# Hi and lo token parts side by side: one 512-column product in the gate and up stage of a decoder layer, Trainium2, one core

## The chip, the cores and the metric

The kernel runs on one core of a Trainium2 chip. The metric is the device time of one execution in microseconds (us). Matrix products run on TensorE (PE; PEld are its weight loads), elementwise work on VectorE (DVE) and ScalarE (ACT); GpSimd (POOL) and SyncE (SP) issue most transfers.

## What is computed

One decoder layer, float32, 512 tokens, width 1024: three token mixers, their gated merge, and a SwiGLU feed-forward part. The change lies in the feed-forward part (F = 2816):

```python
h = h + rms_norm(mix, ln_mix_post)
u = rms_norm(h, ln_ffn_pre)
a = silu(u @ w_gate) * (u @ w_up)          # 1024 -> F, twice
ffn = a @ w_down                           # F -> 1024
h = h + rms_norm(ffn, ln_ffn_post)
```

## The kernel before

Precision. Each float32 matrix x is split into two fp32r tiles: hi is a cast of x by ACT, lo = x - hi by DVE (`split`). A product is three matmuls into one PSUM place: hi hi, hi lo, lo hi (`mm3`).

Seven products. Gate and up products, and the down products behind them, are done on 2 x 2 quarters with seven products in place of eight. The token factors B11, T1, N2, N22, T3, B21, T4 (`fac`; sums and differences of the quarters of the normed tokens) are made once, by `place`. The weights are streamed: the feed-forward width is cut into HF = 11 blocks n, and in each block the products p1, p5, p6, p3, p7, p2, p4 (`PROD`) form one **unit** each: 128 x 1024 weights, that is 2 output groups j of 4 chunks k. Each of these 8 places is an `mm3` of 256 token columns, 24 matmuls a unit (`gu`). j = 0 and 1 fill the two halves of one PSUM bank of 512 columns. p1, p6, p7, p4 add up in the block's bank x, p5 and p3 in y, p2 in w.

A unit's end (`g_end`). After p1, p5 and p6 ACT copies the bank to SBUF (`snap`). After p3, p7 and p2 one DVE op joins the bank with such a copy (`join`). After p4 the activation reads the bank itself. Each finished quarter goes through `act_out`: Silu on ACT (`sg`), a DVE multiply with the up half (`aq`). After all blocks 42 down units follow, with products of 512 columns (`down`, `dn_mm`, `dn_issue`, `dn_sum`).

Order. Weights are loaded by DMAs (SP, some POOL with accumulation), split some units ahead, and multiplied (`Stream`, `fs`). What each engine runs in which order is a table, `ORDER`; `PLAN` gives each tile its place in SBUF or PSUM, so that a reused place makes the next writer wait. All instructions go through one recorder and so carry one line number, L209 (`Noted`). `mix` adds the residual to the mixed tokens: xr = x + mixed, one tile of 128 tokens at a time; xr stays in SBUF up to the end of the kernel, where `dn_half` adds it.

In the trace names lose their numbers: gp is a snapped gate product, hi and lo are the parts of the streamed weights, raw and wide what they are made of. As in the kernel, "block 3" is n = 3.

Of the kernel before, what the change touches and what calls it, by code (L numbers as in the profile page):

```python
# [32 lines left out]
WARM = 10  # L33

# [2027 lines left out]
```

## Time and profile before

| | before |
|---|---|
| time, median of 3 runs (lowest to highest) | 779.85 us (779.32 to 780.1) |
| profiled execution: span, its only own time | 777.5 us |
| PE busy | 769.8 us, 99% |
| DVE busy | 623.0 us, 80% |
| ACT busy | 488.4 us, 63% |
| matmuls and weight loads on PE | 4614 and 4614 |
| gate and up units of blocks 3 to 10 | 504.96 to 666.24 us |
| down units and the last chain | 666.24 us to the end |

The span runs from the first to the last instruction of the one profiled execution; the runs were timed without the profiler and hold what lies around the span too. An engine's busy share is a mean over stages with different limits, so the stage of the change is read by windows and timelines. In a timeline the durations of neighbouring matmuls overlap; what one costs is the step from its start to the next start.

### The profile page before, as it was taken

Reading aid. Unit: us, or ns where it says so; the run is one execution under the profiler, and the core shown is the slowest. Engines: PE = TensorE matmul, PEld = TensorE weight load, DVE = VectorE, ACT = ScalarE, POOL = GpSimd, SP = SyncE. Lnnn points to the kernel's source line nnn. Section 1 sums busy time; section 2 is a strip of 40 time slices with the busy share of each in tenths; the row PEclk is TensorE's granted clock in tenths of the full one; section 3 lists DMA queues with packets and bytes.
Section 4 is the critical chain, followed back from the end, with each engine's and each line's share of the span. In section 5 each row is a group of like instructions: output and inputs, shape, how many; then the busy total and the mean of one; then the engine's idle time right before and its main releaser. Section 6 shows DMA issues by size and latency. Waiting matters only on the chain.

```text
span 777.5 us, 12379 instructions
## 1 busy us (share of the span) xinstructions
PE 769.8 (99%) x4614; PEld 677.3 (87%) x4614; DVE 623.0 (80%) x1003; ACT 488.4 (63%) x881; POOL 100.5 (13%) x133
## 2 busy tenths in 40 slices
PE   9999999999999999999999999999999999999996
PEld 6899888778888888878888899999999999888885
DVE  7994787677787757999898599877776869997776
ACT  7662776678585659778944486455455555766752
POOL 3000421003112020011012001100000000215000
PEclk9999999999999999999999999999999999999999
DMA  8444988248569696478899349877777654949602
GB/s 304 145 127 121 318 258 264 82 154 191 117 138 205 149 200 203 109 193 187 304 341 267 63 109 261 212 181 187 188 190 188 183 146 150 191 103 240 131 1 108
DMA packets 46940, 140.14 MB, mean 180 GB/s; under 512 B 5600, under 2 KB 7184, under 8 KB 46816
## 3 DMA queue, kind: packets, MB, share of 16 engines
q1 hardware_dynamic: 31344, 88.35, 33.8%
q0 software_dynamic: 15104, 50.61, 33.5%
q8 instruction: 36, 0.59, 0.3%
q10 hardware_dynamic: 432, 0.39, 0.2%
q14 instruction: 24, 0.20, 0.1%
HBM read 132.51 MB, written 13.11 MB: 187 GB/s over the span
## 4 chain that ended last, share of the span: by engine, by line
PE 99%; DVE 0%; issue 0%; DVEq 0%; ACT 0%
PE p L209 99%; DVE fg L209 0%; DVEq L2050 0%; DVE s L209 0%; DVE wide L209 0%; ACT sqr L209 0%; DVE eps_t L209 0%
## 5 line engine op out<-in xcount | busy, mean ns | idle before, releaser
L209 DVE TENSOR_TENSOR lo<-raw,hi 128x1024 fp32r<-128x1024 f32 (+3 forms) x140 | 162.5, 1167 | 48.7 <-ACT hi L209 47.4
L209 ACT CAST hi<-raw 128x1024 fp32r<-128x1024 f32 (+3 forms) x140 | 140.5, 1011 | 91.7 <-PE p L209 66.1
L209 ACT CAST hi<-wide 128x1024 fp32r<-128x1024 f32 (+1 forms) x58 | 59.2, 1020 | 54.1 <-PE p L209 27.9
L209 DVE TENSOR_TENSOR lo<-wide,hi 128x1024 fp32r<-128x1024 f32 (+1 forms) x58 | 68.7, 1185 | 17.1 <-ACT hi L209 16.9
L209 PE MATMUL p<-lo,lh 128*128 128x512 f32 x154 | 59.9, 389 | 0.0
L209 PE MATMUL p<-hi,ll 128*128 128x512 f32 x154 | 59.6, 389 | 0.0
L209 PE MATMUL p<-hi,lh 128*128 128x512 f32 x154 | 59.0, 389 | 0.0
L209 PE MATMUL p<-lo,uh 128*128 128x512 f32 (+1 forms) x160 | 57.2, 358 | 0.0
L209 PE MATMUL p<-hi,ul 128*128 128x512 f32 (+1 forms) x160 | 57.0, 358 | 0.0
L209 PE MATMUL p<-hi,uh 128*128 128x512 f32 (+1 forms) x160 | 56.7, 360 | 0.0
L209 PE MATMUL p<-uh,hi 128*128 128x512 f32 x136 | 54.5, 400 | 0.0
L209 PE MATMUL p<-uh,lo 128*128 128x512 f32 x136 | 53.2, 391 | 0.0
L209 PE MATMUL p<-ul,hi 128*128 128x512 f32 x136 | 53.0, 391 | 0.0
L209 POOL DMA_DIRECT2D raw<-in_w_g x24 | 21.0, 879 | 136.8 <-DVE lo L209 109.8
L209 PEld LDWEIGHTS p<-hi,ll 128*128 128x128 f32 x154 | 28.9, 188 | 6.0
L209 PEld LDWEIGHTS p<-lo,lh 128*128 128x128 f32 x154 | 28.9, 188 | 6.0
L209 PEld LDWEIGHTS p<-hi,lh 128*128 128x128 f32 x154 | 28.9, 188 | 5.9
L209 PEld LDWEIGHTS p<-hi,uh 128*128 128x128 f32 x160 | 30.0, 188 | 4.5 <-ACT gq2p L209 0.3
L209 PEld LDWEIGHTS p<-hi,ul 128*128 128x128 f32 x160 | 30.0, 188 | 3.8
L209 PEld LDWEIGHTS p<-lo,uh 128*128 128x128 f32 x160 | 30.1, 188 | 3.6
L209 PEld LDWEIGHTS p<-uh,hi 128*128 128x128 f32 x136 | 25.6, 188 | 6.0 <-issue 0.7
L209 PEld LDWEIGHTS p<-uh,lo 128*128 128x128 f32 x136 | 25.5, 188 | 5.3
(724 smaller groups left out, 2417.7 us busy)
## 6 DMA issues: line engine op xcount, KB each, us to landing
wide<-in_w_gu SPq DMA_DIRECT2D x30, 512.0 KB, 4.7
raw<-in_w_gu SPq DMA_DIRECT2D x27, 512.0 KB, 5.4
raw<-in_w_g POOLq DMA_DIRECT2D x24, 512.0 KB, 6.4
raw<-in_w_g SPq DMA_DIRECT2D x18, 512.0 KB, 4.8
raw<-in_w_p SPq DMA_DIRECT2D x14, 512.0 KB, 5.5
wide<-in_w_gu POOLq DMA_DIRECT2D x14, 512.0 KB, 6.7
raw<-in_w_gu POOLq DMA_DIRECT2D x13, 512.0 KB, 7.6
bp<-in_w_dn SPq DMA_DIRECT2D x22, 256.0 KB, 6.1
```

Source lines behind the costliest of these rows:

```text
L209: ins = f(*args, **kw)
```

## The change

In blocks 3 to 10 a place is two matmuls and not three. The hi and lo tile of each token factor now lie side by side in one tile of 1024 columns (`pair`). The hi part of the weights multiplies 256 columns of the hi tile and 256 of the lo tile in one product of 512 columns, written to two halves of a bank ("main" and "rest"); the lo part of the weights then multiplies the hi columns into main. j = 0 and 1 take a bank each, so a group of products has two banks (`banks`), and the eight banks make four such pairs. Blocks 0 to 2 and the down units keep `mm3`.

At a unit's end ACT copies main (p1, p5, p6 and now p4), and a DVE op adds rest to the copy. A join (p3, p7, p2) becomes two DVE ops, one with main, one with rest, the second reading what the first wrote. p4's activation reads the copy.

To make room in SBUF, xr is written to DRAM by SP after `mix` (`put_away`, 8 writes of 256 KB) and read back in the down stage (`get_back`, 8 reads); the weights of p3 and p7 of the first three down chunks become one tile of 1024 columns, loaded by one transfer and added by one DVE op; two sets of kept products of an earlier stage lie in a spare place. `ORDER` and `PLAN` are new tables.

The core of the diff:

```diff
+    def banks(name):
+        return places.take(psa, "p2", [P, 1024], F32, name)
...
+    def pair(name):
+        t = places.take(ckp, "ck2", [P, 1024], F32R, name)
+        return t[:, :512], t[:, 512:], t[:, :].rearrange("p (s n) -> p s n", s=2)
+
...
+    def put_away(t):
+        away[t] = [drm.tile([P, 512], F32, name=f"h{t}{h}") for h in range(2)]
+        for d, x in zip(away[t], hres[t]):
+            nc.sync.dma_start(d[:, :], x[:, :])
+
+    def get_back(t):
+        hres[t] = [ck(f"hr{t}{h}") for h in range(2)]
+        for d, x in zip(away[t], hres[t]):
+            nc.sync.dma_start(x[:, :], d[:, :])
+
...
     RIGHT = ("B11", "B21", "T1", "N2", "N22", "T3", "T4")
-    fac = {r: Late(lambda c, r=r: (ck(f"{r}h{c}", F32R), ck(f"{r}l{c}", F32R))) for r in RIGHT}
...
+    def banked(n, b):
+
+        return n >= 3
+
+    def halves(ps, i):
+        return ps.rearrange("p (j s n) -> p s j n", j=2, s=2)[:, i]
+
...
         def snap():
             t = ck(f"g{p}{n}")
-            ins = nc.scalar.copy(t[:, :], ps[:, :])
+            ins = nc.scalar.copy(seen(t), main)
             if "behind" in st:
                 after(ins, st["behind"][0])
+            if wide:
+                nc.vector.tensor_tensor(seen(t), seen(t), rest, op=ALU.add)
             gk[(n, p)] = t
-
-        def join(t, x, y, op, i, j):
-            ins = nc.vector.tensor_tensor(t[:, :], x[:, :], y[:, :], op=op)
-            if "behind" in st:
-                after(ins, st["behind"][1])
+            return t
+
+        def join(t, sign, i, j):
+            if sign > 0:
+                ordered_dve(nc.vector.tensor_tensor(seen(t), main, seen(t), op=ALU.add))
+            else:
+                ordered_dve(nc.vector.tensor_tensor(seen(t), seen(t), main, op=ALU.subtract))
+            if wide:
+                nc.vector.tensor_tensor(seen(t), seen(t), rest, op=ALU.add if sign > 0 else ALU.subtract)
             act_out(n, i, j, t[:, :256], t[:, 256:])
 
         if p in ("p1", "p5", "p6"):
             snap()
         elif p == "p3":
-            t = gk.pop((n, "p6"))
-            join(t, t, ps, ALU.subtract, 1, 0)
+            join(gk.pop((n, "p6")), -1, 1, 0)
         elif p == "p7":
-            t = gk.pop((n, "p5"))
-            join(t, t, ps, ALU.subtract, 1, 1)
+            join(gk.pop((n, "p5")), -1, 1, 1)
         elif p == "p2":
-            t = gk.pop((n, "p1"))
-            join(t, ps, t, ALU.add, 0, 0)
+            join(gk.pop((n, "p1")), 1, 0, 0)
+        elif wide:
+            snap()
+            t = gk.pop((n, "p4"))
+            act_out(n, 0, 1, t[:, :256], t[:, 256:], -1.0)
         else:
             act_out(n, 0, 1, ps[:, :256], ps[:, 256:], -1.0)
...
         def gen(hi, lo):
             b = G_BANK[p]
+            wide = banked(n, b)
             if p in ("p1", "p5", "p2"):
-                gb[(n, b)] = dps(f"gw{n}") if b == "w" else aps(f"g{b}{n}")
+                gb[(n, b)] = banks(f"g{b}{n}") if wide else dps(f"gw{n}") if b == "w" else aps(f"g{b}{n}")
             ps = gb[(n, b)]
             for j in range(2):
                 for k in range(4):
-                    r = cols(fac[G_RIGHT[p]][k // 2], (k % 2) * 256, 256)
-                    first = p in ("p1", "p5", "p2") and j == 0 and k == 0
-                    mm3(ps[:, j * 256 : (j + 1) * 256], cols((hi, lo), (j * 4 + k) * P, P), r, first, k == 3)
+                    f = fac[G_RIGHT[p]][k // 2]
+                    begins = p in ("p1", "p5", "p2") and k == 0
+                    w = cols((hi, lo), (j * 4 + k) * P, P)
+                    r = cols(f, (k % 2) * 256, 256)
+                    if wide:
+                        o = ps[:, j * 512 : (j + 1) * 512]
+                        both = f[2][:, :, (k % 2) * 256 : (k % 2 + 1) * 256]
+                        mm(o.rearrange("p (s n) -> p s n", s=2), w[0], both, begins, False)
+                        mm(o[:, :256], w[1], r[0], False, k == 3)
+                    else:
+                        mm3(ps[:, j * 256 : (j + 1) * 256], w, r, begins and j == 0, k == 3)
                 yield 1.44
             g_end(p, n, ps)
...
+            else:
+                rb[(p, c)] = rb.pop(("p3", c))
+                nc.gpsimd.dma_start(rb[(p, c)][:, :], src, accum_op=ALU.add)
...
+                t = rb[("p3", c)]
+                nc.vector.tensor_tensor(rr[c][:, :], rr[c][:, :], t[:, :], op=ALU.add)
+                return
             for i, t in enumerate(rb[("p3", c)]):
...
+
+    for t in range(NT):
+        load_at(len(seq) + units.index(("p2", 1 if t < 2 else 5)), get_back, t)
```

The order on PE at the first product of block 3 (out<-moving, stationary operand as the order prints them: bank0 is PSUM, pair5 the two parts of B11). Before:

```order
L209 MATMUL p1_105<-B11h0_4032,hi3_79 128x256
L209 MATMUL p1_105<-B11l0_4033,hi3_79 128x256
L209 MATMUL p1_105<-B11h0_4032,lo3_83 128x256
L209 MATMUL p1_105<-B11h0_4032,hi3_79 128x256
L209 MATMUL p1_105<-B11l0_4033,hi3_79 128x256
L209 MATMUL p1_105<-B11h0_4032,lo3_83 128x256
```

and in the changed kernel:

```order
L215 MATMUL bank0_104<-pair5_110,hi3_79 128x512
L215 MATMUL bank0_104<-pair5_110,lo3_83 128x256
L215 MATMUL bank0_104<-pair5_110,hi3_79 128x512
L215 MATMUL bank0_104<-pair5_110,lo3_83 128x256
L215 MATMUL bank0_104<-pair3_108,hi3_79 128x512
L215 MATMUL bank0_104<-pair3_108,lo3_83 128x256
```

Two matmuls, of 512 and 256 columns, stand where three of 256 stood.

The order on DVE at the start of block 4 (gpPN is product P of block N: gp14 is p1, gp54 p5, gp64 p6; lo are the parts of the next units' weights; ll1, sq, sr belong to the down products). Before:

```order
L209 TENSOR_TENSOR lo0_80<-raw0_72,hi1_77 128x1024
L209 TENSOR_TENSOR lo2_82<-wide0_84,hi0_76 128x1024
L209 TENSOR_TENSOR lo3_83<-wide0_84,hi3_79 128x1024
L209 TENSOR_TENSOR lo1_81<-wide0_84,hi2_78 128x1024
L209 TENSOR_TENSOR gp64_5186<-gp64_5186,p2_106 128x512
L209 TENSOR_TENSOR lo0_80<-raw1_73,hi1_77 128x1024
```

and in the changed kernel:

```order
L215 TENSOR_TENSOR lo0_80<-wide0_84,hi1_77 128x1024
L215 TENSOR_TENSOR gp14_4982<-gp14_4982,bank0_104 128x512
L215 TENSOR_TENSOR lo2_82<-raw0_72,hi0_76 128x1024
L215 SCALAR_TENSOR_TENSOR aq011_4791<-gp43_4952,sg301_4955 128x256
L215 TENSOR_TENSOR ll1_6096<-aq001_4759,lh1_6095 128x512
L215 TENSOR_TENSOR lo3_83<-wide0_84,hi3_79 128x1024
L215 TENSOR_TENSOR gp54_5005<-gp54_5005,bank0_104 128x512
L215 TENSOR_TENSOR sq1_4958<-aq101_4695,aq111_4728 128x512
L215 TENSOR_TENSOR sr1_4961<-sq1_4958,aq001_4759 128x512
L215 TENSOR_TENSOR gp64_5028<-gp64_5028,bank0_104 128x512
L215 TENSOR_TENSOR lo1_81<-wide0_84,hi2_78 128x1024
L215 TENSOR_TENSOR gp64_5028<-gp64_5028,bank0_104 128x512 x2
```

Before, DVE has nothing to do at the ends of p1, p5 and p6; its first op on block 4's banks is the join that follows p3 (gp64). Now the adds of rest for gp14, gp54 and gp64 stand between the splits, with the squares and the multiply of block 3 before and behind them, and the join is two ops.

The order on SP, where the first weights of the gate and up stage are loaded. Before:

```order
L209 DMA bc_g_fpre1_3691<-in_g_fpre 128x512
L209 DMA raw0_72<-in_w_gu 128x1024
L209 DMA raw2_74<-in_w_gu 128x1024
L209 DMA raw1_73<-in_w_gu 128x1024
L209 DMA raw3_75<-in_w_gu 128x1024
L209 DMA wide0_84<-in_w_gu 128x1024 x5
L209 DMA raw0_72<-in_w_gu 128x1024
```

and in the changed kernel:

```order
L215 DMA raw0_72<-in_w_gu 128x1024
L215 DMA wide0_84<-in_w_gu 128x1024 x4
L215 DMA h00_3755<-xr00_3597 128x512
L215 DMA h01_3756<-xr01_3598 128x512
L215 DMA wide0_84<-in_w_gu 128x1024
L215 DMA raw3_75<-in_w_gu 128x1024
L215 DMA h10_3868<-xr10_3601 128x512
L215 DMA h11_3869<-xr11_3602 128x512
L215 DMA h20_3955<-xr20_3605 128x512
L215 DMA h21_3956<-xr21_3606 128x512
```

The writes of xr (h00 to h31) stand between the loads.

## Rows read from the trace of the kernel before

**Rows 1.** The page, part 1: busy time, share of the span and instructions of each engine.
```profile
PE 769.8 (99%) x4614; PEld 677.3 (87%) x4614; DVE 623.0 (80%) x1003; ACT 488.4 (63%) x881; POOL 100.5 (13%) x133
```

**Rows 2.** The chain of waits in order of time: start us, us, what.
```profile
1.35 769.81 PE p L209 x4613
```

**Rows 3.** Windows: stretch us, its length, busy us of each engine, PEclk, DMA share, GB/s.
```profile
504.96:646.08 141.12, 141.12 (x1179) 141.12 (x1178) 105.55 (x125) 72.24 (x101) 10.48 (x12) 1.00 0.66 176
666.24:771.16 104.92, 104.91 (x464) 86.54 (x462) 87.27 (x141) 67.11 (x117) 18.25 (x21) 1.00 0.56 123
```

**Rows 4.** DVE groups in 504.96 to 666.24: busy us, mean ns | idle before, releasers.
```profile
L209 DVE TENSOR_TENSOR lo<-wide,hi 128x1024 fp32r<-128x1024 f32 x31 | 37.9, 1224 | 15.6 <-ACT hi L209 15.5
L209 DVE TENSOR_TENSOR lo<-raw,hi 128x1024 fp32r<-128x1024 f32 x26 | 31.8, 1225 | 13.7 <-ACT hi L209 13.7
```

**Rows 5.** PE timeline, block 2: start us, us, engine line op out<-in.
```profile
480.00 0.28 PE L209 MATMUL p<-N22h,hi 128*128 128x256 f32 x1
480.12 0.28 PE L209 MATMUL p<-N22l,hi 128*128 128x256 f32 x1
```

**Rows 6.** PE timeline, products of 512 columns, an earlier stage.
```profile
199.99 0.39 PE L209 MATMUL p<-hi,y10h 128*128 128x512 f32 x1
...
201.12 0.39 PE L209 MATMUL p<-hi,y11l 128*128 128x512 f32 x1
```

**Rows 7.** PE timeline, moving operand of two runs (qas).
```profile
176.80 0.28 PE L209 MATMUL p<-kas,qas 128*128 128x256 f32 x1
...
177.39 0.28 PE L209 MATMUL p<-kal,qas 128*128 128x256 f32 x1
```

**Rows 8.** DVE timeline, block 3.
```profile
523.18 0.68 DVE L209 TENSOR_TENSOR gp<-p,gp 128x512 f32<-128x512 f32 x1
523.78 0.68 DVE L209 TENSOR_TENSOR sq<-aq,aq 128x512 f32<-128x512 f32 x1
524.45 1.23 DVE L209 TENSOR_TENSOR lo<-raw,hi 128x1024 fp32r<-128x1024 f32 x1
525.59 0.42 DVE L209 TENSOR_TENSOR aq<-gp,sg 128x256 f32<-128x256 f32 x1
525.93 0.42 DVE L209 SCALAR_TENSOR_TENSOR aq<-p,sg 128x256 f32<-128x256 f32 x1
```

**Rows 9.** ACT timeline from the end of the T1 product, 551.04, of block 5.
```profile
551.12 1.05 ACT L209 CAST hi<-raw 128x1024 fp32r<-128x1024 f32 x1 [0.97 <-PE p L209]
552.07 0.58 ACT L209 COPY gp<-p 128x512 f32<-128x512 f32 x1
```

**Rows 10.** DVE timeline of the same place.
```profile
552.20 1.23 DVE L209 TENSOR_TENSOR lo<-raw,hi 128x1024 fp32r<-128x1024 f32 x1 [0.79 <-ACT hi L209]
```

**Rows 11.** A join of block 2: the next unit on PE, and the join on DVE.
```profile
499.20 0.28 PE L209 MATMUL p<-B21h,hi 128*128 128x256 f32 x1
...
499.40 0.69 DVE L209 TENSOR_TENSOR gp<-gp,p 128x512 f32<-128x512 f32 x1 [0.36 <-PE p L209]
```

**Rows 12.** The first gate products on PE, and DVE beside them.
```profile
442.77 0.39 PE L209 MATMUL p<-B11h,hi 128*128 128x256 f32 x1
...
444.29 0.39 PE L209 MATMUL p<-B11l,hi 128*128 128x256 f32 x1
444.51 0.28 PE L209 MATMUL p<-B11h,lo 128*128 128x256 f32 x1
...
443.81 0.42 DVE L209 TENSOR_TENSOR B11l<-p,B11h 128x256 fp32r<-128x256 f32 x1
```

**Rows 13.** SP loads around the mixing stage, and the first and last residual adds.
```profile
408.95 1.60 SPq L209 DMA_DIRECT2D raw<-in_w_gu  x2
...
453.87 2.40 SPq L209 DMA_DIRECT2D raw<-in_w_gu  x2
...
411.58 1.29 DVE L209 TENSOR_TENSOR xr<-xr,mt 128x512 f32<-128x512 f32 x2
...
445.79 1.28 DVE L209 TENSOR_TENSOR xr<-xr,mt 128x512 f32<-128x512 f32 x2
```

More of the change, by code (lines that the diff above doesn't have):

```diff
@@ L33 @@
 WARM = 10
+PAIRS = 14
+SINGLES = 73 - 2 * PAIRS
 ORDER = {
     "tensor": (
[17 rows of a table removed]
[16 rows of a table added]
     ),
     "vector": (
[32 rows of a table removed]
[33 rows of a table added]
     ),
     "scalar": (
[28 rows of a table removed]
[27 rows of a table added]
     ),
     "gpsimd": (
-        "5-12 16 29-30 4 2-3 0-1 14 13 15 17 22 27 21 20 19 18 23 28 25 24 26 31 33 32 34 39 35 41 40 36 42-43 37 "
-        "47-48 44 38 49-50 45 52 51 53 46 54-65 67 66 68-81 86 82 85 87 83-84 88-111 123-128 119 112-118 120-122"
+        "5-12 16 29-30 4 2-3 0-1 14 13 15 17 22 27 21 20 19 18 23 28 25 24 26 31 33 32 34 39 35 41 40 36 42-43 37 47-48 "
+        "44 38 49-50 45 52 51 53 46 54-65 67 66 68-78 80 79 81-83 86 85 84 87-111 120-125 116 112-115 117-119"
     ),
@@ L125 @@
         "0-14 16-18 15 19-27 32 28-31 33-34 36-38 35 39-52 57 60 53-56 63-64 58-59 61-62 65-94 97-98 95-96 101-102 "
-        "99-100 105-106 103-104 109 107-108 110-218"
[3 rows of a table added]
     ),
@@ L130 @@
     "raw": (
-        "3 2 1 0 3 2 1 0 3 2 1 0 3 2 1 0 3 2 1 0 3 2 1 0 3 2 1 0 3 2 1 0 3 2 1 0 3 2 1 2 1 2 1 0 3 0 3 0 3 2 0 1 3 "
-        "2 0 1 3 2 3 2 3 2 0 3 1 2 0"
+        "3 2 1 0 3 2 1 0 3 2 1 0 3 2 1 0 3 2 1 0 3 2 1 0 3 2 1 0 3 2 1 0 3 2 1 0 3 2 1 2 1 2 1 0 3 0 3 0 3 2 0 1 3 2 0 "
+        "1 3 2 3 2 3 2 0 3 1 2 0"
     ),
     "hi": (
-        "3 2 1 0 3 2 1 0 3 2 1 0 3 2 1 0 3 2 1 0 3 2 1 0 3 2 1 0 3 2 1 0 3 2 1 0 2 3 1 0 2 3 1 0 2 3 1 0 2 3 1 0 2 "
-        "3 1 0 2 3 1 0 2 3 1 0 2 3 1 0 2 3 1 0 2 3 1 0 2 3 1 0 2 3 1 0 2 3 1 0 2 3 1"
+        "3 2 1 0 3 2 1 0 3 2 1 0 3 2 1 0 3 2 1 0 3 2 1 0 3 2 1 0 3 2 1 0 3 2 1 0 2 3 1 0 2 3 1 0 2 3 1 0 2 3 1 0 2 3 1 "
+        "0 2 3 1 0 2 3 1 0 2 3 1 0 2 3 1 0 2 3 1 0 2 3 1 0 2 3 1 0 2 3 1 0 2 3 1"
     ),
     "lo": (
-        "3 2 1 0 3 1 2 0 3 1 2 0 3 1 2 0 3 1 2 0 3 1 2 0 3 1 2 0 3 1 2 0 3 1 0 2 1 3 0 2 1 3 0 2 1 3 0 2 1 3 0 2 1 "
-        "3 0 2 1 3 0 2 1 3 0 2 1 3 0 2 1 3 0 2 1 3 0 2 1 3 0 2 1 3 0 2 1 3 0 2 1 3 0"
+        "3 2 1 0 3 1 2 0 3 1 2 0 3 1 2 0 3 1 2 0 3 1 2 0 3 1 2 0 3 1 2 0 3 1 0 2 1 3 0 2 1 3 0 2 1 3 0 2 1 3 0 2 1 3 0 "
+        "2 1 3 0 2 1 3 0 2 1 3 0 2 1 3 0 2 1 3 0 2 1 3 0 2 1 3 0 2 1 3 0 2 1 3 0"
     ),
     "p": (
[5 rows of a table removed]
[4 rows of a table added]
+    ),
+    "p2": (
+        "0 1 2 3 2 1 0 3 2 3 2 0 1 0 0 3 2 1 0 2 3 3 2 1"
     ),
     "ck": (
[21 rows of a table removed]
[19 rows of a table added]
+    ),
+    "ck2": (
+        "5 3 2 11 7 0 9 13 10 4 12 6 1 8"
     ),
     "s": (
[3 rows of a table removed]
[3 rows of a table added]
     ),
     "spare": (
-        "4 3 2 1 1 4 3 2"
+        "0 1 2 3 4 5 6 7 4 5 0 1"
     ),
     "fraw": (
-        "0 2 1 3 8 7 6 5 4 0 2 1 3 8 0 7 4 5 3 6 1 0 2 8 7 5 6 4 3 1 2 7 0 8 5 4 1 6 3 2 0 5 7 8 4 6 2 1 3 0 7 4 5 "
-        "8 6 1 0 2 3 7 5 6 4"
+        "8 3 1 2 0 6 7 4 5 8 3 1 2 0 8 6 5 7 4 2 1 8 3 0 6 7 2 5 4 1 3 6 8 0 7 5 1 2 4 3 8 7 6 0 5 2 3 1 4 8 6 5 7 0 2 "
+        "1 8 3 4 6 7 2 5 0 1 8"
     ),
     "fhi": (
[3 rows of a table removed]
[3 rows of a table added]
     ),
     "flo": (
[3 rows of a table removed]
[3 rows of a table added]
     ),
@@ L243, in __init__, with open @@
         self.held, self.used = {}, 0
-    def open(self, pool, kind, n, shape):
+    def open(self, pool, kind, n, shape, dt=F32):
         for i in range(n if PLAN else 0):
             key = f"{kind}{i}"
-            self.held[key] = pool.tile(shape, F32, tag=key, name=key, bufs=1)
+            self.held[key] = pool.tile(shape, dt, tag=key, name=key, bufs=1)
     def fixed(self, pool, shape, dt, name):
@@ L265, in take @@
         n = int(next(self.plan[kind]))
+        if kind == "ck" and n < SINGLES:
+            return pool.tile(shape, dt, tag=f"ck{n}", name=name, bufs=1)
         if kind == "ck":
-            return pool.tile(shape, dt, tag=f"ck{n}", name=name, bufs=1)
+            n -= SINGLES
+            return self.held[f"pair{n // 2}"][:, n % 2 * 512 : n % 2 * 512 + 512]
+        if kind == "ck2":
+            return self.held[f"pair{n}"]
+        if kind in ("p", "p2"):
+            return self.held["bank0"][:, n * shape[1] : (n + 1) * shape[1]]
         if kind == "spare":
-            return self.held["wide0"][:, self.spare + n * 512 : self.spare + (n + 1) * 512]
+            o = self.spare + n * 512 + (300 if n > 6 else 0)
+            return self.held["wide0"][:, o : o + 512]
         if kind == "fraw" and n > 3:
@@ L353, in tile_kernel @@
     base = ctx.enter_context(tc.tile_pool(name="base", bufs=1))
-    ckp = ctx.enter_context(tc.tile_pool(name="ckp", bufs=73))
+    ckp = ctx.enter_context(tc.tile_pool(name="ckp", bufs=SINGLES))
     sm = ctx.enter_context(tc.tile_pool(name="sm", bufs=16))
@@ L367, in tile_kernel @@
     places.open(sm, "s", 16, [P, 8])
-    places.open(psa, "p", 8, [P, 512])
+    places.open(psa, "bank", 1, [P, 8 * 512])
+    places.open(ckp, "pair", PAIRS, [P, 1024], F32R)
     def ck(name, dt=F32):
         return places.take(ckp, "ck", [P, 512], dt, name)
+    def pair(name):
+        t = places.take(ckp, "ck2", [P, 1024], F32R, name)
+        return t[:, :512], t[:, 512:], t[:, :].rearrange("p (s n) -> p s n", s=2)
     def small(name, n=4):
@@ L790, in q_end @@
         if p in ("p1", "p5", "p6", "p7"):
-            t = qkeep[(p, i)] = ck(f"gq{b}{p}{i}")
+            t = qkeep[(p, i)] = (spare if b == SWA and p in ("p1", "p6") else ck)(f"gq{b}{p}{i}")
             st["chain"] = nc.scalar.copy(t[:, :], ps[:, :])
@@ L1474, in x_load @@
             nc.sync.dma_start(hres[t][h][:, :], a["x"][t * P : (t + 1) * P, h * 512 : (h + 1) * 512])
+    away = {}
+    def put_away(t):
[6 more added lines that the diff above has]
+            nc.sync.dma_start(x[:, :], d[:, :])
     mixed = {}
@@ L1504, in mix @@
             )
+        put_away(t)
         return tmp
     RIGHT = ("B11", "B21", "T1", "N2", "N22", "T3", "T4")
-    fac = {r: Late(lambda c, r=r: (ck(f"{r}h{c}", F32R), ck(f"{r}l{c}", F32R))) for r in RIGHT}
+    fac = {r: Late(lambda c, r=r: pair(f"{r}{c}")) for r in RIGHT}
     turned = {}
@@ L1532, in place @@
         for c in range(2):
-            h, l = (x[:, :].rearrange("p (k n) -> p k n", k=2)[:, :, o : o + P] for x in fac[name][c])
+            h, l = (x.rearrange("p (k n) -> p k n", k=2)[:, :, o : o + P] for x in fac[name][c][:2])
             v = src[:, c * 256 : (c + 1) * 256].rearrange("p (k n) -> p k n", k=2)
@@ L1644, in tile_kernel, with seen, ordered_dve @@
     G_RIGHT = dict(p1="B11", p5="T1", p6="N2", p3="N22", p7="T3", p2="B21", p4="T4")
+    def banked(n, b):
+        return n >= 3
+    def halves(ps, i):
+        return ps.rearrange("p (j s n) -> p s j n", j=2, s=2)[:, i]
     def g_end(p, n, ps):
+        b = G_BANK[p]
+        wide = banked(n, b)
+        main = halves(ps, 0) if wide else ps[:, :].rearrange("p (j n) -> p j n", j=2)
+        rest = halves(ps, 1) if wide else None
+        def seen(t):
+            return t[:, :].rearrange("p (j n) -> p j n", j=2)
+        def ordered_dve(ins):
+            if "behind" in st:
+                after(ins, st["behind"][1])
         def snap():
             t = ck(f"g{p}{n}")
-            ins = nc.scalar.copy(t[:, :], ps[:, :])
+            ins = nc.scalar.copy(seen(t), main)
             if "behind" in st:
                 after(ins, st["behind"][0])
+            if wide:
+                nc.vector.tensor_tensor(seen(t), seen(t), rest, op=ALU.add)
             gk[(n, p)] = t
-        def join(t, x, y, op, i, j):
-            ins = nc.vector.tensor_tensor(t[:, :], x[:, :], y[:, :], op=op)
-            if "behind" in st:
-                after(ins, st["behind"][1])
+            return t
[6 more added lines that the diff above has]
+                nc.vector.tensor_tensor(seen(t), seen(t), rest, op=ALU.add if sign > 0 else ALU.subtract)
             act_out(n, i, j, t[:, :256], t[:, 256:])
@@ L1684, in gen @@
             b = G_BANK[p]
+            wide = banked(n, b)
             if p in ("p1", "p5", "p2"):
-                gb[(n, b)] = dps(f"gw{n}") if b == "w" else aps(f"g{b}{n}")
+                gb[(n, b)] = banks(f"g{b}{n}") if wide else dps(f"gw{n}") if b == "w" else aps(f"g{b}{n}")
             ps = gb[(n, b)]
@@ L1724, in tile_kernel @@
     LAST = 3
+    RAW3 = 3
     rr = {}
@@ L1751, in dn_issue @@
                 nc.gpsimd.dma_start(rr[c][:, :n], src, accum_op=ALU.add)
+        elif p in ("p3", "p7") and c < RAW3:
+            src = a["w_dn"][:, h, j * HF + ks[0] : j * HF + ks[-1] + 1].rearrange("p k n -> p (k n)")
+            if p == "p3":
+                rb[(p, c)] = places.take(fp, "fraw", [P, 1024], F32, f"q{c}")
+                nc.sync.dma_start(rb[(p, c)][:, :], src)
+            else:
+                rb[(p, c)] = rb.pop(("p3", c))
+                nc.gpsimd.dma_start(rb[(p, c)][:, :], src, accum_op=ALU.add)
         elif p == "p7":
@@ L1762, in add @@
         def add():
+            if c < RAW3:
+                t = rb[("p3", c)]
+                nc.vector.tensor_tensor(rr[c][:, :], rr[c][:, :], t[:, :], op=ALU.add)
+                return
             for i, t in enumerate(rb[("p3", c)]):
```

223 rows, old and new, of tables (ORDER, PLAN) are left out of this document.

## The prediction, before the run

> **What bounds the kernel now.** I read the engine totals, then the chain, then the windows of the stage that the change touches, then single instructions there. PE is busy 99% of the span, DVE 80% [rows 1]. The chain of waits is one piece of PE matmuls, 769.81 us long, with nothing between them [rows 2]. Blocks 3 to 10 run from 504.96 to 666.24, which is 20.16 us a block and 2.88 a unit; in the first seven of them PE fills all 141.12 us at granted clock 1.00, DVE works 105.55 of these and ACT 72.24 [rows 3]. So each ns taken from PE's stream there is worth a ns, until PE has to wait for a bank; DVE, with 5.1 us idle a block, is the next limit. Over the eight blocks 15.6 + 13.7 us of DVE's idle time are waits for ACT's hi cast [rows 4].
>
> **What PE gains.** A matmul of 256 columns starts every 120 ns [rows 5]. One of 512 columns starts every 226.6 ns: from 199.99 to 201.12 are five steps [rows 6]. 256 more columns cost 106.6 ns, so 13.4 ns of each matmul are independent of its length. The change streams the same columns and has one matmul and one weight load fewer in each of 8 blocks x 7 units x 8 places = 448 places: a place takes 226.6 + 120 = 346.6 ns instead of 360. A unit becomes 2.773 us, a block 19.41, and the gain is 448 x 13.3 = **6.0 us**. The new moving operand is two runs, a row of no 512-column product here; the nearest has 256 columns in two runs of 128 (kas times qas) and comes every 116 to 120 ns like the plain ones [rows 7], so I price this form at nothing.
>
> The Trainium skill (TensorE: Matmul & The Clock Gate, section "Wait — 56ns, not 53.3ns?") puts the fixed cost of a warm matmul at about 2.5 ns; by that, an estimate, merging would return only 1.1 us. The two pitches above do not agree with it, and the sum goes by them.
>
> **What DVE and ACT pay.** Each unit's end now leaves two halves in PSUM, and the second needs a DVE add of 512 columns. Such an op lasts 0.68 us, but the next one starts 0.60 after it (523.18, 523.78) [rows 8]. Seven adds a block are 4.2 us; on 15.1 (105.55 over seven) that is 19.3. Counting the changed order's own rows from one p2 join to the next, with pitches 1.14, 0.60 and 0.34 for 1024, 512 and 256 columns [rows 8], gives 18.7 on average: some squares and sums now stand behind the last block. Three of the seven adds (joins of p3, p7, p2) read what the op ahead of them has just written, so they start at its end plus about 0.03: 0.72 instead of 0.60, 0.36 a block. Together **19.05 of 19.41 us**: DVE is full to 98%, where it was 75%. Were the pitch between 0.60 and the whole 0.68 on all 24.7 ops of a block, it would be up to 2.0 more; I take 0.60, since it is measured on this form.
>
> The Trainium skill (VectorE: DVE Perf Modes, section "The DRAIN you can't avoid") says that the next op does not start until the pipe is empty. By that, the upper bound just named would hold and the kernel would be slower (case C below); the rows show starts 0.08 before the previous end, and so do not agree.
>
> ACT gains one copy a block (p4; a copy is 0.58 [rows 9]): 72.24 us of 141.12 become 76 [rows 3], hidden.
>
> **The wait that is added.** A unit's bank pair may be overwritten only when the rest add has read it. Four pairs are in turn, and most products write where one stood two units before. Take a unit that ends at T. ACT casts the next weights first (T+0.08), copies the product from T+1.03 to T+1.61 [rows 9]. DVE stands in its fixed order: lo, which waited for that cast, starts at T+1.16 [rows 10] and holds it 1.14, so the rest add runs from T+2.30 to T+2.98. The next-but-one unit wants the bank at T+2.77: **0.2 to 0.25 us late**. Before, the bank was free at T+1.61, or, for a join, which starts 0.20 after the unit (499.40 for 499.20) [rows 11], at about T+0.9. In the other case of the order shown above, block 4's p5, DVE has lo, the p1 add, lo, a multiply, ll, lo ahead of the add; it gets to it 0.68 late. When PE does wait, its next matmuls also lose about 0.09: 444.29 waits for the DVE op from 443.81 (end 444.23), and 444.51 comes 0.22 later instead of 0.12 [rows 12].
>
> I laid the changed order's rows one behind another with these durations for all eight blocks. A stall at one boundary relieves the next, so they are eleven and not fifty-six: five of 0.24 or 0.25 (p1 and p6 of block 3, p6 of 5, p5 of 7, p1 of 8), two of 0.68 (p5 of 4 and 6), 0.11, 0.09, 0.44 and 0.64 in blocks 8 to 10. That is 3.8 us, and 11 x 0.09 = 1.0: **4.8 us given back**. The order of before, laid in the same way, has no stall, as in the trace. The bounds: nothing, if the adds come a third of an op earlier; and DVE's whole pace, below.
>
> **The rest.** DVE does more behind block 10: it is busy 87.27 of 104.92 us there [rows 3], about 5 more fit, and the laid rows give PE no wait; taken at nothing, and up to 1 us if that work falls into a stretch where DVE is already full. The eight writes of the residual stand in SP's queue among the gate and up loads, each behind its tile's add. Two loads that SP issued at 408.95 now wait for the tile added from 411.58 to 412.87 [rows 13]: 4 us later, against a first gate product at 442.77 [rows 12]; the last writes are ready at 445.79 + 1.28 = 447.07, before SP's next load at 453.87 [rows 13]. Nothing, unless the writes hold up a load that is needed at once; then a few tenths. The reads back are 2 MB in the last 105 us, where the DMAs are busy 0.56 [rows 3]. Fewer, larger bp loads and one add of 1024 (1.14) for two of 512 (1.20) are too small to see. Rows before block 3 are swapped in a few places on DVE; I put -0.3 to +0.6 on that and take nothing.
>
> **Sum.** -5.97 + 4.84 = -1.1. The profiled execution's span of 777.5 becomes 776.4; the median of the runs lies 2.35 above that span, and so the time is **778.7** against 779.85.
>
> **Rivals.** 0.2% is 1.56 us, about what a measurement of this kernel can tell from no change: faster is below 778.29, slower above 781.41.
>
> A. As summed, most of the gain returned as PE waits of 0.1 to 0.7 us. Its own range, 777.0 to 780.6, is stalls of 3.1 to 6.7. Chance 0.48, of which 0.14 is faster, 0.32 the same, 0.02 slower.
>
> B. The adds come in time. For it: the plain case fails by a quarter of a us only, and one early stall relieves those after it; against it: the fixed order puts a 1.14 us lo ahead of each add. With no stall 773.9, with half of them 776.3. Chance 0.28, faster.
>
> C. DVE sets the pace, and the kernel is **slower**. It is 19.05 us busy a block; it waits 5.1 now, 3.7 of it for ACT's cast ((15.6 + 13.7) / 8) [rows 4]. The cast itself waits for PE to free its hi tile, 0.97 us ahead of 551.12 [rows 9], so each PE stall passes to ACT and back to DVE. The same end is reached if the ops take their whole 0.68: 18.7 + 2.0 = 20.7 a block, 784.2. It decides at 20.16 - 19.05 = 1.1 us of idle left a block; my laid rows have 0.96, which is close. With 1.6 left, a block takes 20.65 and the time is 779.85 + 8 x 0.49 = 783.8; range 781.5 to 785. Against it: a DVE that is late finds its inputs ready, and its waits shrink. Chance 0.19.
>
> D. Merging saves little, because 512 columns in two runs lose a few ns at the turn, or the fixed part is not per matmul. If 2 to 3 ns of the 13.4 fall away, 1.1 us are gained; the stalls shrink as the units stay longer, to six of some 0.2: 779 to 780.5. Against it are the pitches of [rows 5, 6, 7]. Chance 0.05, 0.04 the same and 0.01 slower. The Trainium skill's fixed cost, quoted above from TensorE: Matmul & The Clock Gate, would be this case.
>
> **Numbers.** Faster: 0.14 + 0.28 = 0.42. Same: 0.32 + 0.04 = 0.36. Slower: 0.02 + 0.19 + 0.01 = 0.22. The range has to hold most of B and half of C: 774.0 to 782.5.
>
> **What would show it.** In the profile after: matmuls in blocks 3 to 10 alternate 226.6 and 120 ns; units without a wait take 2.77 us; DVE is busy over 18.5 of each 20 us there; PE's gaps, 0.1 to 0.7 us and some eleven in all, stand at unit starts and end when a DVE add on a bank ends, most behind p1, p5 and p6; up to 504.96 and from block 10's end the times are those of before, moved. If a lone 512-column product takes 240 ns, D holds. If PE's gaps sum to under 2 us, B holds. If they sum to over 7.5 with DVE waiting for hi in between, C. I am wrong in another way if the difference lies before 504.96 (a late load) or in the last 105 us.

## The result, and the profile after

| | before | after |
|---|---|---|
| time, median of 7 runs each | 779.65 us | 781.79 us |
| ratio (95% interval) | | 1.0027 (1.0016 to 1.0038) |
| span of the profiled execution | 777.5 us | 779.7 us |
| blocks 3 to 10 | 161.28 us | 161.34 us |

The changed kernel is 0.27% slower; the forecast was 778.7 us, 1.1 us faster. The page's engine totals after, which answer to [rows 1]:

```profile
PE 769.2 (99%) x4166; PEld 653.4 (84%) x4166; DVE 655.9 (84%) x1050; ACT 492.9 (63%) x883; POOL 97.8 (13%) x130
```

PE has 448 matmuls fewer and is still busy for the same time (769.8 us before). The windows after (columns as in [rows 3]): blocks 3 to 10, their first seven, the down units.

```profile
506.22:667.56 161.34, 159.54 (x898) 136.83 (x897) 153.08 (x197) 93.74 (x134) 12.21 (x14) 1.00 0.66 176
506.22:647.60 141.38, 139.77 (x787) 119.87 (x786) 133.40 (x171) 78.37 (x110) 10.47 (x12) 1.00 0.67 179
667.56:772.50 104.94, 104.91 (x464) 86.53 (x462) 91.01 (x142) 63.30 (x106) 15.78 (x18) 1.00 0.61 142
```

The two spans differ by 2.2 us, and the stage of the change has hardly a share in it: it starts 1.26 later (506.22 for 504.96), lasts 0.06 longer; the down units take the same 104.52 to the last matmul (770.76 before, 772.08 after); the end behind that takes 7.62 us for 6.77 (the spans to the hundredth are 779.71 and 777.53). DVE works 133.40 us in seven blocks, 19.06 a block. The chain of waits, one piece before [rows 2], has 167 pieces now. From the start of block 3 and of the last wait of block 4 (start us, us, what):

```profile
504.94 4.17 PE bank L215 x27
509.11 0.02 issue
509.13 1.07 ACT hi L215
510.20 0.02 issue
510.22 1.23 DVE lo L215
511.45 0.61 DVE gp L215
512.06 0.04 issue
512.10 1.44 PE bank L215 x7
...
533.20 0.60 DVE ll L215
533.80 1.14 DVE lo L215
534.93 0.61 DVE gp L215
535.54 0.04 issue
535.59 18.42 PE bank L215 x105
```

The first wait is the plain case of the prediction: p1's unit ends at 509.1, ACT casts, DVE subtracts, then adds rest, and p6's first product starts at 512.10. The second is block 4's p5. PE and DVE timelines there:

```profile
534.17 0.39 PE L215 MATMUL bank<-pair,hi 128*128 128x512 f32 x1
534.40 0.28 PE L215 MATMUL bank<-pair,lo 128*128 128x256 f32 x1
534.51 0.39 PE L215 MATMUL bank<-pair,hi 128*128 128x512 f32 x1
534.75 0.28 PE L215 MATMUL bank<-pair,lo 128*128 128x256 f32 x1
535.59 0.50 PE L215 MATMUL bank<-pair,hi 128*128 128x512 f32 x1 [0.56 <-DVE gp L215]
535.92 0.28 PE L215 MATMUL bank<-pair,lo 128*128 128x256 f32 x1
```

```profile
531.64 1.22 DVE L215 TENSOR_TENSOR lo<-raw,hi 128x1024 fp32r<-128x1024 f32 x1
532.78 0.42 DVE L215 SCALAR_TENSOR_TENSOR aq<-gp,sg 128x256 f32<-128x256 f32 x1
533.11 0.69 DVE L215 TENSOR_TENSOR ll<-aq,lh 128x512 fp32r<-128x512 f32 x1
533.72 1.22 DVE L215 TENSOR_TENSOR lo<-wide,hi 128x1024 fp32r<-128x1024 f32 x1
534.85 0.68 DVE L215 TENSOR_TENSOR gp<-gp,bank 128x512 f32<-128x512 f32 x1
```

That DVE queue is the one the order showed, op for op, and the last product before the wait would end its step at 534.87; the next starts at 535.59. A wait is counted wherever PE's step from one product to the next is over 0.05 us longer than 0.2267 (512 columns) or 0.12 (256 columns); what the steps have above these sums to 4.3 us in the stage. So 4.2 us of PE time were gained (161.28 less 157.1, the stage without its waits) and 4.3 given back.

### The profile page after: what moved, and what is told of

Its sections match the earlier page's. It is cut to its first block, busy times and chain, and to the rows that moved or that the text cites. A ratio compares the mean times of both kernels' runs of the same rounds, so it can differ in the third digit from the quotient of the medians.

```text
span 779.7 us, 11519 instructions
## 1 busy us (share of the span) xinstructions
PE 769.2 (99%) x4166; PEld 653.4 (84%) x4166; DVE 655.9 (84%) x1050; ACT 492.9 (63%) x883; POOL 97.8 (13%) x130
## 4 chain that ended last, share of the span: by engine, by line
PE 90%; DVE 6%; issue 2%; ACT 2%; DVEq 0%
PE bank L215 90%; DVE lo L215 3%; DVE gp L215 2%; DVE wide L215 1%; ACT hi L215 1%; ACT mw L215 0%; DVE aq L215 0%; DVE pair L215 0%; ACT L215 0%; ACT wide L215 0%; ACT pair L215 0%; DVE fg L215 0%; ACT mt L215 0%; DVEq L2136 0%; DVE sq L215 0%
## 5 line engine op out<-in xcount | busy, mean ns | idle before, releaser
L215 PE MATMUL bank<-pair,hi 128*128 128x512 f32 (+1 forms) x1072 | 309.9, 360 | 1.8 <-DVE gp L215 1.5
L215 PE MATMUL bank<-pair,lo 128*128 128x256 f32 (+1 forms) x768 | 230.3, 300 | 0.0
L215 PEld LDWEIGHTS bank<-pair,hi 128*128 128x128 f32 x1072 | 189.8, 189 | 36.1 <-DVE gp L215 4.8
L215 PE MATMUL bank<-hi,pair 128*128 128x512 f32 (+1 forms) x694 | 213.0, 376 | 0.0
L215 PEld LDWEIGHTS bank<-pair,lo 128*128 128x128 f32 x768 | 145.4, 189 | 5.3
L215 PEld LDWEIGHTS bank<-hi,pair 128*128 128x128 f32 x694 | 127.7, 188 | 23.0 <-ACT gq2p L215 0.4
L215 PE MATMUL bank<-lo,pair 128*128 128x512 f32 (+1 forms) x352 | 132.3, 376 | 0.0
L215 PEld LDWEIGHTS bank<-lo,pair 128*128 128x128 f32 x352 | 66.1, 188 | 10.8
L215 DVE TENSOR_TENSOR gp<-gp,bank 128x512 f32<-128x512 f32 x78 | 53.3, 684 | 3.4 <-PE bank L215 1.7
L215 DVE TENSOR_TENSOR_SCAN bw<-br,bw 128x512 f32<-128x512 f32 (+3 forms) x32 | 24.3, 808 | 4.6 <-ACT bw L215 4.5
```

The source lines that it names most:

```text
L215: ins = f(*args, **kw)
```

## The experiments

A short notation: "stage" is blocks 3 to 10, from the first product of block 3 to the first down product; "waits" is counted as above; "tail" runs from the start of the last matmul to the end of the span. The kernel before was timed beside each group (779.6 to 779.85). A time without an interval is of one run, but for the first row's.

| kernel | time us | ratio (95%) | stage from, length | waits | tail |
|---|---|---|---|---|---|
| before | 779.65 | | 504.96, 161.28 | 0 | 6.77 |
| before2 | 779.85 | | 505.50, 161.28 | 0 | 6.77 |
| after | 781.79 | 1.0027 (1.0016 to 1.0038) | 506.22, 161.34 | 4.3 | 7.62 |
| tail | 781.29 | 1.0022 (1.0013 to 1.0031) | 506.70, 161.63 | 3.8 | 6.94 |
| earlyp | 782.73 | 1.0035 (1.0021 to 1.0048) | 507.24, 161.77 | 4.1 | 7.63 |
| bothfirst | 779.47 | 0.9999 (0.9990 to 1.0007) | 507.21, 158.74 | 1.4 | 7.63 |
| copyfirst | 792.49 | one run | 506.76, 171.53 | 14.6 | 7.63 |
| onerun | 782.0 | one run | 506.10, 161.58 | 4.1 | 7.62 |
| grouped | 780.96 | 1.0016 (1.0006 to 1.0025) | 506.84, 160.10 | 3.1 | 7.63 |
| grouped8 | 781.16 | one run | 506.91, 159.94 | 3.5 | 7.63 |
| p1only | 778.62 | 0.9983 (0.9973 to 0.9993) | 506.06, 158.71 | 1.2 | 6.95 |
| shifted | 778.68 | 0.9990 (0.9980 to 0.9999) | 506.17, 159.01 | 1.2 | 6.95 |
| best1 | 777.79 | 0.9974 (0.9964 to 0.9983) | 506.39, 158.01 | 1.6 | 6.94 |
| best2 | 777.71 | 0.9972 (0.9961 to 0.9984) | 505.71, 158.05 | 1.6 | 6.94 |

### Is it the rest add's place in DVE's order? bothfirst and copyfirst

Edit of bothfirst: at 19 places DVE's order has the rest add ahead of the split it stood behind, and at 23 places ACT has the copy ahead of the cast. Nothing else. Of block 5:

```diff
 vector
-729 728 730 731 732 734 733
+729 728 731 730 732 733 734
 scalar
-609 610 611 710 613 612 615 614
+610 609 611 710 612 613 614 615
```

> The changed kernel with two orders turned round at the ends of p1, p5 and p6 in blocks 3 to 10: ACT copies the product ahead of the cast of the next weights, and DVE adds the rest ahead of the split that it stands behind. Nothing is added or left out. Theory (the waits of PE come from the place of the adds in the queues): laid one behind another the waits fall from ten with 3.1 us (4.5 with what each restart costs) to six with 0.85 (1.4): the stage falls from 161.3 to about 158.3, the time from 781.8 to about 778.8. Rival (DVE sets the pace, 19.06 us of 20.2 a block, whatever its order): DVE waits longer for the copies, the waits move to the weights' splits, and the time stays at 781 or rises.

The stage is 2.6 us shorter than in the change, the waits fall from 4.3 to 1.4 us, and the time is that of the kernel before. DVE did the same work (busy 152.61 us in this stage, 153.08 in the change's), so two thirds of the waits were made by the order, and not by DVE's load. copyfirst moves ACT's copies alone, and leaves DVE's adds behind the splits:

> The changed kernel with ACT's copy ahead of the cast of the next weights at the ends of p1, p5 and p6 in blocks 3 to 10, and DVE's order left alone: half of the run before, and the half that alone should harm. Theory (DVE stands in its order): the split ahead of each add now waits for a cast that comes half a microsecond later, and the add behind it comes later too though its copy is ready earlier; laid one behind another PE waits 17 times, 12.4 us (13.9 with the restarts) instead of 3.1: the stage grows from 161.3 to about 170, the time to 790. Rival (what matters is how early ACT's copy is done): the waits shrink and the time falls below 781.

14.6 us of PE waits, 13.9 laid. A late cast delays the split, and the add stands behind that. Two lines of the waits view of copyfirst's stage (engine, line, waited for: us, times, longest), and DVE's timeline at one of these waits; that DVE's own waits for the cast come to 14.6 us too is chance:

```profile
DVE lo L128 <- ACT hi L128: 14.6, 16, 2.0
PE bank L128 <- DVE gp L128: 6.5, 10, 0.9
```

```profile
533.06 1.23 DVE L128 TENSOR_TENSOR lo<-wide,hi 128x1024 fp32r<-128x1024 f32 x1 [1.25 <-ACT hi L128]
534.20 0.68 DVE L128 TENSOR_TENSOR gp<-gp,bank 128x512 f32<-128x512 f32 x1
```

DVE stood idle for 1.25 us, waiting for the cast, with an add behind it whose copy had been made at 532.08. An engine's order, not its load, decided in both runs, in opposite directions. DVE's adds moved alone were not run.

### What does the merged place cost? onerun, grouped, grouped8

onerun reads the moving operand as one run of 512 columns (the hi tile) in place of two runs:

```diff
-both = f[2][:, :, (k % 2) * 256 : (k % 2 + 1) * 256]
-mm(o.rearrange("p (s n) -> p s n", s=2), w[0], both, begins, False)
+both = f[0]
+mm(o, w[0], both, begins, False)
```

> The changed kernel with a moving operand of one run: the 512-column product reads 512 neighbouring columns of the hi tile instead of 256 of hi and 256 of lo (so the hi weights times lo tokens are left out, and wrong columns added in their place; all counts and sizes stay). The changed kernel's place takes 233 + 117 = 350 ns where 226.6 + 120 = 346.6 was forecast. Theory A, the turn between the two runs costs it: the steps become 226.6 and 120, units without a wait 2.773 us, the stage 1 to 1.5 us shorter less what the waits grow. Theory B, changing between 512 and 256 columns costs it: the steps stay 233 and 117 and the stage stays at 161.3.

The kernel leaves out a product that is needed and adds a wrong one in its place, so its time alone counts. Two runs cost nothing that shows: stage and waits are within 0.3 us of the change's. grouped changes the order in a unit: four products of 512 columns, then four of 256, per group j. grouped8: eight and eight.

```diff
-for k in range(4):
+for s, k in ((s, k) for s in range(2 if wide else 1) for k in range(4)):
...
+    if s == 0:
         mm(o.rearrange("p (s n) -> p s n", s=2), w[0], both, begins, False)
+    else:
         mm(o[:, :256], w[1], r[0], False, k == 3)
```

> The changed kernel with the matmuls of each half unit in another order: four of 512 columns, then four of 256, instead of alternating. Theory B, changing size costs 3.4 ns a place: only one change of each kind is left in four places, so the mean place falls from 350 to about 347.5, a unit by 20 ns, the stage by up to 1.1 us, of which the waits take some back: 781 to 781.8. Theory A, the two runs cost it: the steps between 512-column products read 229 to 233, the mean place stays 350, the time 781.8.

> The changed kernel with each unit's matmuls in the order eight of 512 columns, then eight of 256. In the run with four and four the 512-column steps stayed at 233 ns (226.7 in the down stage), and the first five 512-column steps behind block 10 read 0.23 to 0.24 too, in the kernel before as well. Theory: a 512-column product costs 233 for some five matmuls behind a run of 256-column ones and then 226.7, so that the mean 512-column step falls to about 231 here, and a unit by some 20 to 25 ns. Rival: 233 belongs to this product (its operands) and stays for all eight.

In grouped the stage without its waits is 157.0 us, as in the change (157.1): the gain is fewer waits. In grouped8 it is 156.4. There every undisturbed unit is alike, eight products of 512 columns in 1.84 us and eight of 256 in 0.95 (PE timeline):

```profile
540.49 1.11 PE L128 MATMUL bank<-pair,lo 128*128 128x256 f32 x8
541.45 2.00 PE L128 MATMUL bank<-pair,hi 128*128 128x512 f32 x8
543.29 1.11 PE L128 MATMUL bank<-pair,lo 128*128 128x256 f32 x8
544.24 1.55 PE L128 MATMUL bank<-pair,hi 128*128 128x512 f32 x6
```

From 541.45 to 543.29 the mean step of a 512-column product is 0.230. One by one the eight are 0.233, 0.236, 0.228, 0.233, 0.231, 0.227, 0.227, 0.227: behind a run of 256-column products the first five take more than the 0.2267 of [rows 6].

### Two paces: p1only and shifted

With that I went back to the trace of the change and took the mean place between any two waits. In its stretches of 15 to 62 places it has two values and none between: 0.3467, the predicted one, and 0.3533. In the quick pace the two steps are 0.230 and 0.117, and not the forecast 0.2267 and 0.12; only their sum is the forecast one. From 506.22 to 511.52, 15 places, and from 518.56 to 534.51, 46 places:

```profile
506.22 0.40 PE L215 MATMUL bank<-pair,hi 128*128 128x512 f32 x1
...
511.52 0.40 PE L215 MATMUL bank<-pair,hi 128*128 128x512 f32 x1
...
518.56 0.40 PE L215 MATMUL bank<-pair,hi 128*128 128x512 f32 x1
```

5.30 / 15 = 0.3533; 15.95 / 46 = 0.3467 (the row of 534.51 stands above). A stretch keeps its pace to its end; the pace changes where PE waits, in either direction. In the six kernels with alternating places the first stretch of block 3 had 0.3533 each time, and over the stage the two mix, somewhat over half slow in the change, most of it in tail (mean places of 0.3506 and 0.3524). In p1only p1 of each block has its eight and eight, and the six other units alternate; in shifted each 256-column product comes one place later. Both have the orders of bothfirst and tail.

```diff
 p1only
-for s, j in ((s, j) for s in range(2 if wide else 1) for j in range(2)):
+for s, j in ((s, j) for s in range(2 if wide and p == "p1" else 1) for j in range(2)):
...
+if s == 1 or p != "p1":
...
 shifted
+late.append((o[:, :256], w[1], r[0], False, k == 3))
+if len(late) > 1:
+    mm(*late.pop(0))
...
+if j and wide:
+    mm(*late.pop(0))
```

> Base: the changed kernel with the rest adds and copies ahead (bothfirst) and the output writes in the old order (tail). Only p1 of each block has its eight 512-column products first and its eight 256-column ones behind; p5 to p4 alternate as in the change. In the traces so far the alternating places have two steady paces, 0.3467 us (what the prediction took) and 0.3533, and keep one from one PE wait to the next; entered from the 256-column stream of block 2 it was 0.3533 in every kernel. Theory S (the pace is set by the matmuls that stand just ahead): p1 ends in eight 256-column products, so every p5 is entered as block 3 was, and the stretches from p5 to the next wait have 0.3533 in all eight blocks; p1 itself takes 2.793 us. Stage 8 x 2.793 + 392 x 0.352 + waits of 1.4 = 161.7 at most, 159 to 160 if half the stretches behind waits are quick. Rival W (the pace changes only when PE has waited): the pace on both sides of a p1 unit without a wait is the same, quick or slow. Rival P (any break in the pattern draws it anew): behind p1 quick in some blocks, slow in others, with no wait between.

> Base as in p1only. In every unit of blocks 3 to 10 each 256-column product stands one place later, behind the 512-column product of the next place: a unit is two 512-column products, then 256 and 512 in turn, then two 256-column ones at its end. Theory S: all units that begin without a wait have one and the same pace, since the same four matmuls stand ahead of each; if it is the quick one, the stage is 448 x 0.3467 + waits of 1.5 to 2.5 = 157 to 158 and the time 776.5 to 777.5; if the slow one 160 and 779.5. Rival W: the paces change only at waits, as in the kernels before, first stretch 0.3533, and the stage is 158.5 to 159.5. Rival P: units differ with no wait between.

In p1only every p5 has 0.3533, in all eight blocks, also in the blocks 7 and 9, whose p1 came after units at 0.3467. On PE p2, p4 of block 6 and p1, p5 of block 7, and the start of p6:

```profile
580.05 0.39 PE L128 MATMUL bank<-pair,hi 128*128 128x512 f32 x1
...
582.82 0.39 PE L128 MATMUL bank<-pair,hi 128*128 128x512 f32 x1
...
585.59 0.39 PE L128 MATMUL bank<-pair,hi 128*128 128x512 f32 x1
...
588.39 0.40 PE L128 MATMUL bank<-pair,hi 128*128 128x512 f32 x1
...
591.22 0.40 PE L128 MATMUL bank<-pair,hi 128*128 128x512 f32 x1
```

Units of 2.77, 2.77, 2.80 (eight and eight) and 2.83 us, and no wait between. So theory S holds for an entry from eight 256-column products: what stands just ahead sets the slow pace each time, and rivals W (only a wait changes it) and P (drawn anew) fall for it. In shifted most undisturbed units are 2.818 and 2.822 in turn, near the slow value. The quick pace hoped for came behind a wait of 0.04 in block 10 (656.40), and once against S: p2 of block 4 takes 2.79 us, behind a p7 in the slow pace and with no wait between that the trace shows, as P had it:

```profile
540.43 0.63 PE L128 MATMUL bank<-pair,hi 128*128 128x512 f32 x2
...
543.22 0.63 PE L128 MATMUL bank<-pair,hi 128*128 128x512 f32 x2
```

So the matmuls just ahead do not settle the pace in every order, and what brings the quick one, there and behind a wait, stays open.

### The start and the end: before2, earlyp, tail

before2 is the kernel before once more, to see how far its own marks scatter. earlyp takes the places in PSUM for everything up to block 3 from the plan of before; tail exchanges two output writes at the end of SP's order.

```diff
 earlyp: PLAN "p", its first 214 places
-those of the change
+those of before
 tail: sync, the end
-228 230 229 231
+228 229 230 231
```

> The kernel before, unchanged, profiled a second time, to see how much of its early part is scatter. In the profiled executions the first product of block 3 starts at 504.96 before and at 506.22, 506.70, 506.10, 506.84 and 507.21 in the changed kernel and four kernels made from it, which have the same instructions up to there. Theory (part of it is systematic): this profile shows again 115.5 us from PE's 1620th to its 2170th matmul (the others 116.1 to 116.3) and 60.9 us from its 2300th to block 3 (the others 61.1); what it has before the 1620th, 302.6, may move by some tenths. Rival (all scatter): these stretches read 116 and 61.1 here too.

> The changed kernel with the PSUM places of the kernel before for every bank that is taken ahead of block 3 (the first 214 of the table's places for p; the tables of the order and of SBUF stay). Theory (renumbered banks make PE or the engines behind it wait in the mixer stages): the 116.2 us from the 1620th to the 2170th matmul become 115.5 and the 61.1 from the 2300th to block 3 become 60.9: the time falls by 0.6 to 0.9, to about 781.0. Rival (the changed order or the places in SBUF make the difference): stretches and time stay, 781.8.

> The changed kernel with two neighbours in SP's queue exchanged at the very end: the write of tile 2's second half stands again ahead of the write of tile 3's first half, as in the kernel before. Theory: in the changed kernel three output writes of 256 KB land after the last DVE op instead of two, and the third costs about 0.7 us (256 KB at 380 GB/s). Expected: span and time fall by 0.6 to 0.8 us against the changed kernel (781.79 to about 781.1), last matmul still near 772.1. Rival: the 0.9 us by which the end came later behind the last matmul is scatter of the drain; then the time stays at 781.8.

The first marks of a run scatter: block 3 starts at 504.96 and 505.50 in two traces of the same kernel, and over all traces PE reaches its 1620th matmul 302.6 to 303.6 us into the span. Most of what is left is steady (bothfirst's profile lost 1.2 us more at 419.5 to 421.3, where ACT had waited for a load). From PE's 1620th to its 2170th matmul the kernel before takes 115.54 and 115.59, the changed one and its kin 116.14 to 116.26, earlyp 115.61. Half of it is found at the transposes of the router, which write eight results into PSUM. Before, then after:

```profile
310.43 1.04 PE L209 MATMUL p<-c_ident,mw 128*128 128x128 f32 x8
311.22 0.47 PE L209 MATMUL p<-hi,y02h 128*128 128x512 f32 x1
```

```profile
311.08 1.34 PE L215 MATMUL bank<-c_ident,mw 128*128 128x128 f32 x8
312.17 0.47 PE L215 MATMUL bank<-hi,y02h 128*128 128x512 f32 x1
```

0.79 before and 1.09 after, to the next product. Another 0.2 stands just ahead, where two products take 0.66 (from 308.80) for 0.46 before. So the new plan's places cost 0.6 us in this stretch; earlyp, which changes nothing but places, gives them back, but its seam with the rest of the new plan makes another wait of 1.1 us (454.43, PE for DVE's gp), and it is slower as a whole. best2 hands over earlier and has the 0.6 without that wait. Another 0.2 us lies from the 2300th matmul to block 3 (60.9 before, 61.1 in all others, and 62.2 in earlyp with its wait). It is one step, at the first gate products. In the new order DVE makes t, which it made at 446.99 before, ahead of a B11 lo part that [rows 12] has at 443.81, and the product with that part comes 0.32 behind the one ahead of it, at 445.23, for 0.12 before:

```profile
444.48 0.68 DVE L215 TENSOR_TENSOR t<-bank,ur 128x512 f32<-128x512 f32 x1
445.08 0.41 DVE L215 TENSOR_TENSOR pair<-bank,pair 128x256 fp32r<-128x256 f32 x1
```

```profile
445.55 0.39 PE L215 MATMUL bank<-pair,hi 128*128 128x256 f32 x1
```

This is read from the traces; no run put t back.

At the end, before, after and tail, on SP:

```profile
773.80 0.99 SPq L209 DMA_DIRECT2D out<-fg  x2
```

```profile
775.12 1.31 SPq L215 DMA_DIRECT2D out<-fg  x3
```

```profile
773.14 0.33 SPq L128 DMA_DIRECT2D out<-fg  x1
```

In the change one finished tile's write stood behind the write of a tile not yet ready, so three writes leave at the very end. In tail it leaves at 773.14, with two left for the end (from 775.88), and the end behind the last matmul is 6.94 for 7.62 us, the time 0.5 lower. The 0.17 by which 6.94 is over the 6.77 of before stays open.

### Together: best1 and best2

best1 is bothfirst, grouped8 and tail; best2 has, besides, the first 189 PSUM places of before.

> The three edits that the runs so far speak for, together: copies and adds first at the ends of p1, p5 and p6 (as in bothfirst), each unit's matmuls as eight of 512 and eight of 256 columns (as in grouped8), and SP's last writes in the old order (as in tail). Theory: the stage takes 56 units of 2.796 us = 156.6 and some six waits with 0.9 (1.4 with the restarts), 158.0 instead of 161.3, and the end 0.66 less: 781.8 - 3.3 - 0.7 = 777.8, faster than the kernel before (779.7) by 1.9. Rival (DVE, 19.06 us busy of the 19.6 that are left a block, gives out): the stage stays above 159.5 and the time above 779.

> The same, and with the PSUM places of the kernel before for the first 189 banks, that is up to the mixing stage (earlyp had them up to block 3, which cured the stretch from the 1620th to the 2170th matmul and brought a new wait of 1.1 us at 454). Theory: 115.6 us in that stretch instead of 116.2 and no new wait at 454: 0.6 us less than the run beside it, about 777.2. Rival: the hand-over at another place makes another wait, and the time is the same as beside it or longer.

Both beat both kernels: 0.26 to 0.28% under the kernel before, 0.5% under the change. best2's start (505.71) is the earlier one, but the two times differ by 0.08 only, within their intervals: the 0.6 that its trace has is not shown by the times. The stage of best1:

```profile
506.39:664.40 158.01, 157.92 (x898) 138.13 (x897) 152.30 (x196) 93.49 (x135) 12.25 (x14) 1.00 0.68 179
```

DVE is busy 152.30 of 158.01 us, 96%, and PE waits for 1.6 us only.

## Why the prediction was wrong, by its own steps

**PE's gain, 6.0 us: mis-sized, 4.2 measured.** The forecast pace, 0.3467, exists and runs for 46 places on end. But I took two pitches from streams of one width each [rows 5, 6] and added them up, and in the alternation PE holds 0.3533 for more than half of the places. Stage less waits, 157.1, is 448 x 0.3506. With the prediction's 106.6 ns for 256 columns, the part of a matmul that does not go by its length is 13 ns in the quick pace and 17 in the slow one. The Trainium skill (TensorE: Matmul & The Clock Gate, section "Wait — 56ns, not 53.3ns?") states a fixed cost of about 2.5 ns for a warm matmul; neither pace agrees. **Rival D**, a gain of 1.1 us, falls with the 4.2 measured, and onerun takes away one of its grounds, the two runs; its direction, that merging saves less than the two pitches say, was right.

**Waits, 4.8 us: right.** 4.3 us, at ten of the eleven boundaries named (the eleventh, p1 of block 9, is 0.04); the two long ones, p5 of 4 and 6, lose 0.84 - 0.12 = 0.72 plus 0.1 behind it, where 0.68 and 0.09 were laid. In blocks 8 to 10 the waits are shorter than laid. Laying DVE's fixed order by measured pitches gave the changed kernel, copyfirst (13.9, measured 14.6) and the stage of best1.

**DVE's work, 19.05 us a block: right.** 19.06. So the pitch of 0.60 holds, and 534.85 starts 0.09 before 533.72 + 1.22. The sentence that the prediction took from the Trainium skill (VectorE: DVE Perf Modes, section "The DRAIN you can't avoid") is half of what stands there: the section adds that a next op that is not held starts earlier, and with that the rows agree.

**Rival C (DVE sets the pace): right in its sign, wrong in its mechanism.** The kernel is slower, but DVE's wait for the cast fell from 15.6 + 13.7 us [rows 4] to

```profile
L215 DVE TENSOR_TENSOR lo<-wide,hi 128x1024 fp32r<-128x1024 f32 x33 | 40.2, 1220 | 2.8 <-ACT hi L215 2.8
L215 DVE TENSOR_TENSOR lo<-raw,hi 128x1024 fp32r<-128x1024 f32 x24 | 29.3, 1219 | 2.4 <-ACT hi L215 2.4
```

as was argued against it, and best1 does the same DVE work at 96% in 158.0 us. **Rival B**, the adds in time, did not come of itself; bothfirst made it by order, with 1.4 us of waits left, and still took 779.47, since the slow pace and both ends stayed.

**"The rest": a term put at nothing, 1.7 measured.** The early part, which I put at -0.3 to +0.6 and took at nothing, costs 0.8: I did not look at which PSUM place each early tile gets in the new plan (0.6), and did not follow what one of the swapped DVE rows does to the first gate products (0.2). The end costs 0.85 and was in no term: I stopped at the last matmul and did not read SP's order behind it, which is 0.68 of it. The down units are unchanged, as said.

In sum: -4.2 + 4.3 + 0.8 + 0.85 = +1.8; the spans differ by 2.2, and the other 0.4 lies ahead of the 1620th matmul (302.64 and 303.06 us), where the two traces of the kernel before differ as much (302.64 and 303.12). Against the forecast of -1.1, +1.8 came from the pace, -0.6 from the waits, +1.7 from start and end. So two steps failed, the pace and the rest, each large enough to take the forecast gain away; that the waits came out within 0.6 us was not luck, as the same laying gave copyfirst, bothfirst and best1 too.
